# Two of four weight sums of a unit by accumulating transfers, and gelu as one function, in the projection stage of a one-core decoder layer

## The chip, the cores and the metric

The kernel runs on one core of a Trainium2 chip. The metric is the device time of one execution in microseconds; the median of three runs counts. Engines are named as in the profile: PE is TensorE, DVE VectorE, ACT ScalarE, POOL GpSimd, SP SyncE, which here only issues DMAs.

## The reference

One decoder layer for a prompt of 1024 rows and eight single decode rows, all float32, width 1024. What matters here is its first line and the recurrent branch:

```python
z = x @ w_in
xr, yr, q, k, v, xq, g = jnp.split(z, SPLIT_IDX, axis=-1)
xc, conv_new = causal_conv(xr, conv_buf, conv_w, conv_b)
hs, h_new = rg_lru(xc, h0, lru_wa, lru_ba, lru_wx, lru_bx, lru_lambda)
a_out = hs * jax.nn.gelu(yr, approximate=True)
```

`w_in` has 1024 rows and 7680 columns, cut among two halves of the recurrent branch (`xr`, `yr`), queries, keys and values of the window attention, queries of the memory attention, and three sets of gates. Two attention branches, the merge by gates, two layer norms and a gated feed-forward part follow; the change does not touch them.

## The kernel before

**Products.** Activations lie transposed: 1032 columns (1024 prompt rows and 8 decode rows) on 128 partitions by 8 blocks. Each float32 operand is split into a high and a low float32r part (`split`: a cast on ACT, then a subtraction on DVE), and each product is three matmuls (high by high, high by low, low by high).

**Units.** The first stage, `project`, works through 30 units (`UNITS`). A unit makes two blocks of 128 columns of `z` from two blocks of `w_in`, with seven products of half size where the plain way has eight. Its weights are four quarters, a11 and a12 (the halves of the first block, 128 x 512 each) and a21 and a22 (of the second). The seven weight operands, numbered 0 to 6, are

    0: a11          1: a21 + a22     2: (1) + a11    3: a12
    4: a11 + a21    5: (2) + a12     6: a22

So four of them (1, 2, 4, 5) are sums. `fast_load` loads the quarters of a unit from HBM on SP's queue (tiles `ur`), `fast_quarter` makes operand i (its sum into a tile `us`, on DVE, and its split into `u_ih` and `u_il`), and `fast_step` runs its 24 matmuls (two halves of the columns, four blocks, three matmuls each) into PSUM banks `ub`, `uc` or `ud` and copies the result out: `p1s`, `p5s` and `u2s` on ACT for i = 0, 1, 2, `za` and `zb` on DVE for i = 3, 4, 5, `zb` on ACT for i = 6. Operands 0, 2, 4, 6 add to the same bank `ub`, so step 2 starts only when `p1s` is copied, step 4 when `u2s` is, and step 6 when DVE has made `zb`.

**Order.** The loop in `project` asks for operand k + 3 at step k, three steps ahead. Loads of unit u + 1 are asked for in steps 1 to 3 of unit u. Behind each step, `pump` advances side work by a piece: the recurrent branch of a `lru` unit (`lru`: convolution, gates, a scan on DVE, gelu, a store to `scr_a`), memory attention of the decode rows (`dec_mem`: dot products `dcj` on DVE with tiles `dck`, `dcv` and broadcast rows `dckq`, `dcvq`), and others. From the seventh step on, a scheduler sets each engine's order by its own costs; before that it is as written. POOL has little to do in the stage: small copies of the recurrent branch (`pconv`, `scvo`, `pho`, `sho`) and one pass over `tr` per `lru` unit.

**Buffers.** Tiles `ur` have the tag `raw` with 6 buffers, tiles `us` the tag `sum` with 3 buffers in this stage (`sum_bufs`). A unit u > 1 is loaded in pieces (`staged`): two quarters at once, and the other two one by one by `fast_more`.

**Gelu.** `lru` writes gelu as y (1 + tanh(c (y + a y^3))) / 2 with a square and a tanh on ACT and three passes on DVE, the last of which multiplies with the scan's result.

Of the kernel before, what the change touches and what calls it, by code (L numbers as in the profile page):

```python
# [13 lines left out]
AF = mybir.ActivationFunctionType  # L14
ALU = mybir.AluOpType
# [5 lines left out]
D = 1024  # L21
# [29 lines left out]
SHARE = 0.5 / ALPHA  # L51
LN_EPS = 1e-5 / ALPHA ** 2
NEG = -1.0e30
GELU_C = math.sqrt(2.0 / math.pi)
GELU_A = math.sqrt(0.044715)

V_BG, V_CW, V_CB, V_BA, V_BX, V_LAM = 0, 24, 56, 64, 72, 80
V_G1, V_B1, V_G2, V_B2, V_SNK, V_SNKD, V_EPS, V_N = 88, 96, 104, 112, 120, 136, 137, 138
# [2 lines left out]
class Builder:  # L61
# [210 lines left out]

    def fast_load(self, u, src0, src1, staged=False):
        h = D // 2
        parts = [partial(self.half_raw, src[:, e * h:(e + 1) * h], h, f"ur{u}_{j}{e}")
                 for j, src in enumerate((src0, src1)) for e in range(2)]
        st = {"raw": [[f() for f in parts[:2]], []], "u": u, "more": deque(parts[2:])}
        if not staged:
            self.fast_more(st, 2)
        return st  # L280

    def fast_more(self, st, n):

        for _ in range(n):
            st["raw"][1].append(st["more"].popleft()())

    def sum_tile(self):

# [2 lines left out]
    def fast_quarter(self, st, i):  # L291

        nc, u = self.nc, st["u"]
        byhand = self.sfree is not None
        if byhand:
            a11, a12, a21, a22 = (st["r"].get(n) for n in (11, 12, 21, 22))
        else:
            a11, a12 = st["raw"][0]
            a21, a22 = st["raw"][1] or (None, None)
        if i in (1, 2, 4, 5):  # L300
            if byhand:
                src = st[2] if i == 5 else self.sum_tile()
            else:
                src = self.w1.tile([P, D // 2], F32, tag="sum", name=f"us{u}_{i}", bufs=self.sum_bufs)
            a, b = {1: (a21, a22), 2: (st.get(1), a11), 4: (a11, a21), 5: (st.get(2), a12)}[i]
            nc.vector.tensor_add(src, a, b)
            st[i] = src
        else:
            src = {0: a11, 3: a12, 6: a22}[i]
        if byhand and i == 2:  # L310
            self.sfree.append(st[1])
        if st.get("fifth") and i == 5:
            if not st["first"]:
                self.raw_done(st, 12)
            return
        hi, lo = self.half_pair(f"u{u}_{i}")
        self.split(hi, lo, src)
        if byhand and i in (4, 5):
            self.sfree.append(src)
        if byhand and i > 3:  # L320
            self.raw_done(st, *{4: (11, 21), 5: (12,), 6: (22,)}[i])
        st["q", i] = hi, lo
# [77 lines left out]
    def project(self, ctx, pool):  # L400

        nc, io, tc = self.nc, self.io, self.tc
        self.qdc = self.cst.tile([P, KT * NB], F32, name="qdc")
        self.qds = self.cst.tile([P, KT * NB], F32, name="qds")
        self.kd = self.cst.tile([P, 2 * NB], F32, name="kd")
        self.vd = self.cst.tile([NB, 256], F32, name="vd")
        self.lru_setup()
        self.side, self.pumped, self.late_gate = (deque(), deque()), 0, None
        n = len(UNITS)
        finish = [Finish(self, kind, j) for kind, j in UNITS]  # L410
        st = {}

        def load(u):
            a, b = finish[u].rows
            st[u] = self.fast_load(u, io["win"][a], io["win"][b], u > 1)

        ts = [[None] * 7, [None] * 7]
        for i in (6, 5, 2, 0, 1, 3, 4):
            for p in range(2):
                ts[p][i] = tuple(self.tp.tile([P, 4, QS], F32R, tag=f"t{i}", name=f"t{e}{i}_{p}", bufs=4) for e in "hl")  # L420
        todo = [(u, i) for u in range(n) for i in range(7)]
        ahead = 3
        xs = {}
        moving = self.combos(ts, xs)
        with tc.manual_schedule(engines=ORDERED):
            with pool("mx") as self.ph:
                self.mem_kv(moving, xs, lambda: load(0), [lambda i=i: self.fast_quarter(st[0], i) for i in range(2)])
            self.fast_quarter(st[0], 2)
            for k, (u, i) in enumerate(todo[:FIRST]):
                if i == 1:  # L430
                    load(u + 1)
                v, j = todo[k + ahead]
                if i == 1:
                    self.fast_step(st[u], i, ts, finish[u])
                if i != 2:
                    self.fast_quarter(st[v], j)
                if i == 2:
                    self.fast_step(st[u], i, ts, finish[u])
                next(moving, None)
                if k < 3:  # L440
                    next(moving, None)
                if i == 2:
                    self.fast_quarter(st[v], j)
                elif i != 1:
                    self.fast_step(st[u], i, ts, finish[u])
        assert next(moving, None) is None
        self.lr = ctx.enter_context(pool("lr"))
        self.dp = ctx.enter_context(pool("dp1"))
        with tc.issue_after(self.last_load):
            self.load_consts()  # L450
            self.load_lru()
        self.lru_consts()
        for k, (u, i) in enumerate(todo):
            if k < FIRST:
                continue
            if i == 1 and u + 1 < n:
                load(u + 1)
            if i in (2, 3) and u + 1 < n:
                self.fast_more(st[u + 1], 1)
            if k + ahead < len(todo):  # L460
                v, j = todo[k + ahead]
                self.fast_quarter(st[v], j)
            self.fast_step(st[u], i, ts, finish[u])
            self.pump()
            if i == 6:
                del st[u]
        while any(self.side):
            self.pump()
        nc.sync.dma_start(self.scr["c"][:, :, TP:T], self.cdec)
        self.store_lru()  # L470
        self.late_gate = None
# [491 lines left out]
    def lru(self, m, xr, yr):  # L963

        nc, io, vec = self.nc, self.io, self.vec
        col = lambda base: vec[:, base + m:base + m + 1]
        stt = nc.vector.scalar_tensor_tensor
# [17 lines left out]
        a, ti = self.zt(f"tr{m}"), self.zt(f"ti{m}")  # L985
        for c, (t0, n) in enumerate(THIRDS):
            x = [self.lr.tile([P, n], F32R, tag=f"xc{e}", name=f"xc{e}{m}_{c}", bufs=1) for e in range(2)]
            for e, r in enumerate(half):
                src = xc[r, t0:t0 + n]
# [18 lines left out]
        sq = self.zt(f"sq{m}")  # L1008
# [12 lines left out]
        nc.gpsimd.tensor_copy(self.sho[:, m, :], sq[:, TP:T])  # L1021
        yield
        g = self.zt(f"ge{m}")
        nc.scalar.activation(g, yr, AF.Square, scale=GELU_A)
        yield
        stt(g, g, 1.0, yr, op0=ALU.add, op1=ALU.mult)
        nc.scalar.activation(g, g, AF.Tanh, scale=GELU_C)
        yield
        stt(g, g, 1.0, yr, op0=ALU.add, op1=ALU.mult)
        yield  # L1030
        stt(g, sq, 0.5, g, op0=ALU.mult, op1=ALU.mult)
        nc.sync.dma_start(self.scr["a"][:, m, :], g)


# [318 lines left out]
    def plain(self, h):  # L1353

        ts = [[None] * 7, [None] * 7]
        steps = self.h_combos(h, ts)
        for f in range(PLAIN):
            self.plain_gate_up(f, h, steps)
        for _ in steps:
            pass  # L1360
        for p in range(2):
            ts[p][0], ts[p][3], ts[p][5] = h[p, 0], h[p, 1], h[2 + p, 1]
        return ts
# [699 lines left out]
class FinishDown:  # L2063


    scale = 1.0 / ALPHA
# [158 lines left out]
```

## Time and profile before

| what | value |
|---|---|
| time, median of 3 runs | 1877.86 us (1877.57 to 1879.27) |
| profiled execution, its own time | 1878.24 us |
| its span in the profile | 1876.5 us |
| granted TensorE clock, mean | 0.998 |
| PE busy | 1856.7 us, 99% of the span |
| DVE busy | 1443.0 us, 77% |
| ACT busy | 1055.0 us, 56% |
| POOL busy | 123.5 us, 7% |

Busy time is the union of an engine's instructions. PE's instructions overlap: a matmul of 128 x 258 is shown with some 0.28 us, and the next one starts 0.12 us after it. In a row of a group, the columns are line, engine, operation, output <- inputs, shape and count, then busy us, mean ns of one, and the engine's idle time just before them with what ended it. In a row of waits they are engine, line, what was waited for, us in total, how often, and the longest.

### The profile page before, as it was taken

The numbers are of one execution on the slowest core, as the hardware profiler recorded it, in microseconds if no ns is written. First come the engines' busy times: TensorE is split into PE (matmuls) and PEld (weight loads), VectorE is DVE, ScalarE is ACT, GpSimd is POOL, SyncE is SP. The second block draws the span as 40 slices with busy tenths as digits, with TensorE's granted clock in tenths as the row PEclk, the third lists the DMA queues.
The fourth block names the chain that finished last, engine by engine and source line by source line (L and its number), as shares of the span: only waits on it lengthen the run. The fifth ranks groups of instructions, "written<-read, shape, count | busy, mean of one in ns | idle before, by whom it ended". The sixth has DMA issues, their size and how long they took to land.

```text
span 1876.5 us, 38122 instructions
## 1 busy us (share of the span) xinstructions
PE 1856.7 (99%) x14616; PEld 1839.8 (98%) x14616; DVE 1443.0 (77%) x2932; ACT 1055.0 (56%) x2250; POOL 123.5 (7%) x187
## 2 busy tenths in 40 slices
PE   9999999999999999999999999999999999999998
PEld 9999999999999999999999999999999999999998
DVE  7878878888789757578887567798888787957486
ACT  6576676665666756568774234644443434735355
POOL 1000002110000000021210000000000000001100
PEclk9999999999999999999999999999999999999999
DMA  9535345447344368547535251255576566967862
GB/s 337 177 109 175 111 145 166 139 139 267 120 159 164 124 203 269 203 134 237 176 93 190 91 192 57 74 170 185 182 242 199 162 197 225 311 181 190 190 197 91
DMA packets 186678, 326.93 MB, mean 174 GB/s; under 512 B 19760, under 2 KB 97536, under 8 KB 186496
## 3 DMA queue, kind: packets, MB, share of 16 engines
q1 hardware_dynamic: 179392, 304.86, 49.4%
q0 software_dynamic: 4224, 14.78, 3.9%
q10 hardware_dynamic: 2880, 4.85, 0.7%
q8 instruction: 115, 1.88, 0.4%
q14 instruction: 67, 0.55, 0.1%
HBM read 238.76 MB, written 89.84 MB: 175 GB/s over the span
## 4 chain that ended last, share of the span: by engine, by line
PE 83%; DVE 6%; DMA 6%; issue 3%; ACT 2%; SPq 0%; POOL 0%; ACTq 0%; DVEq 0%; POOLq 0%
PE ub L332 5%; PE ub L334 5%; PE ub L333 5%; PE ubfg L332 3%; PE ubfg L334 3%; PE ubfg L333 3%; PE ud L334 2%; PE ud L333 2%; PE ud L332 2%; PE op L134 2%; PE op L136 2%; PE op L135 2%; PE brs L145 2%; PE brs L142 2%; PE brs L143 2%
## 5 line engine op out<-in xcount | busy, mean ns | idle before, releaser
L332 PE MATMUL ub<-th,u_6h 128*128 128x258 f32 x240 | 68.5, 285 | 1.4 <-DVE zb L380 1.1
L332 PE MATMUL ub<-th,u_2h 128*128 128x258 f32 x240 | 68.1, 284 | 0.8 <-ACT p1s L373 0.8
L332 PE MATMUL ub<-th,u_4h 128*128 128x258 f32 x240 | 68.2, 284 | 0.3 <-ACT u2s L373 0.3
L334 PE MATMUL ud<-th,u_5l 128*128 128x258 f32 x240 | 68.1, 284 | 0.0
L332 PE MATMUL ud<-th,u_1h 128*128 128x258 f32 x240 | 68.1, 284 | 0.0
L332 PE MATMUL ud<-th,u_5h 128*128 128x258 f32 x240 | 68.1, 284 | 0.0
L332 PE MATMUL ub<-th,u_0h 128*128 128x258 f32 x240 | 68.1, 284 | 0.0
L334 PE MATMUL ub<-th,u_6l 128*128 128x258 f32 x240 | 68.1, 284 | 0.0
L334 PE MATMUL ud<-th,u_1l 128*128 128x258 f32 x240 | 68.1, 284 | 0.0
L334 PE MATMUL ub<-th,u_0l 128*128 128x258 f32 x240 | 68.1, 284 | 0.0
L334 PE MATMUL ub<-th,u_2l 128*128 128x258 f32 x240 | 68.0, 284 | 0.0
L334 PE MATMUL ub<-th,u_4l 128*128 128x258 f32 x240 | 68.0, 284 | 0.0
L334 PE MATMUL uc<-th,u_3l 128*128 128x258 f32 x240 | 68.0, 284 | 0.0
L332 PE MATMUL uc<-th,u_3h 128*128 128x258 f32 x240 | 68.0, 283 | 0.0
L333 PE MATMUL ub<-tl,u_6h 128*128 128x258 f32 x240 | 67.7, 282 | 0.0
L333 PE MATMUL ub<-tl,u_0h 128*128 128x258 f32 x240 | 67.6, 282 | 0.0
L333 PE MATMUL ud<-tl,u_5h 128*128 128x258 f32 x240 | 67.6, 282 | 0.0
L333 PE MATMUL ub<-tl,u_4h 128*128 128x258 f32 x240 | 67.6, 282 | 0.0
L333 PE MATMUL ud<-tl,u_1h 128*128 128x258 f32 x240 | 67.6, 282 | 0.0
L333 PE MATMUL ub<-tl,u_2h 128*128 128x258 f32 x240 | 67.6, 282 | 0.0
L333 PE MATMUL uc<-tl,u_3h 128*128 128x258 f32 x240 | 67.6, 282 | 0.0
L134 PE MATMUL op<-mh,woh 128*128 128x258 f32 x224 | 63.4, 283 | 0.0
(1080 smaller groups left out, 8230.0 us busy)
## 6 DMA issues: line engine op xcount, KB each, us to landing
ur<-win SPq DMA_DIRECT2D x120, 256.0 KB, 3.0
raw<-wgu SPq DMA_DIRECT2D x80, 256.0 KB, 3.4
t<-scr_t SPq DMA_DIRECT2D x36, 516.0 KB, 4.0
z<-scr_f SPq DMA_DIRECT2D x28, 516.0 KB, 5.3
scr_f<-z SPq DMA_DIRECT2D x22, 516.0 KB, 2.9
scr_t<-z SPq DMA_DIRECT2D x20, 516.0 KB, 3.1
raw<-wdn SPq DMA_DIRECT2D x35, 256.0 KB, 5.4
z<-scr_t SPq DMA_DIRECT2D x16, 516.0 KB, 6.2
```

The source lines that it names most:

```text
L134: nc.tensor.matmul(ps, sh, mh, start=opens and i == 0, stop=False)
L135: nc.tensor.matmul(ps, sh, ml, start=False, stop=False)
L136: self.last_mm = nc.tensor.matmul(ps, sl, mh, start=False, stop=closes and i == last).ins
L142: mm(sh, mh, start=opens and i == 0, stop=False)
L143: mm(sl, mh, start=False, stop=False)
L145: self.last_mm = mm(sh, ml, start=False, stop=closes and i == len(terms) - 1).ins
L332: mm(sh[:, w], xh, start=opens and k == 0, stop=False)
L333: mm(sh[:, w], xl, start=False, stop=False)
L334: self.last_mm = mm(sl[:, w], xh, start=False, stop=k == 3).ins
```

## The change

For units 2 to 29, `fast_sums` replaces the loading. Operands 0, 3 and 6 are loaded as they are (a11, a12, a22). For operands 1 and 4 the first summand is loaded on SP's queue into a `sum` tile, and the second is added to it by an accumulating DMA on POOL's queue. Operands 2 and 5 are made by DVE in place in operand 1's tile, which is split again after each. a11, a21 and a22 are thus read twice from HBM. Loads are asked for in steps 1 to 4. The tile of operand 1 is held until operand 5 is split, that of operand 4 until its own split. Gelu is one function of ACT and one product on DVE.

```diff
     def fast_load(self, u, src0, src1, staged=False):
         h = D // 2
+        if staged:
+            return self.fast_sums(u, src0, src1)
...
+    def fast_sums(self, u, src0, src1):
+
+        h, nc = D // 2, self.nc
+        (a11, a12), (a21, a22) = ([src[:, e * h:(e + 1) * h] for e in range(2)] for src in (src0, src1))
+        raw = {}
+
+        def plain(k, src):
+            raw[k] = self.half_raw(src, h, f"ur{u}_{k}")
+
+        def both(k, a, b):
+            raw[k] = self.half_raw(a, h, f"us{u}_{k}", True)
+            nc.gpsimd.dma_start(raw[k], b, accum_op=ALU.add)
+
+        plain(0, a11)
+        both(1, a21, a22)
+        return {"sum": raw, "u": u, "more": deque((partial(plain, 3, a12), partial(both, 4, a11, a21), partial(plain, 6, a22)))}
...
     def fast_quarter(self, st, i):
 
         nc, u = self.nc, st["u"]
+        if "sum" in st:
+            raw = st["sum"]
+            if i in (2, 5):
+                nc.vector.tensor_add(raw[1], raw[1], raw[{2: 0, 5: 3}[i]])
+            hi, lo = self.half_pair(f"u{u}_{i}")
+            self.split(hi, lo, raw[{2: 1, 5: 1}.get(i, i)])
+            st["q", i] = hi, lo
+            return
...
-            if i in (2, 3) and u + 1 < n:
+            if i in (2, 3, 4) and u + 1 < n:
                 self.fast_more(st[u + 1], 1)
...
         g = self.zt(f"ge{m}")
-        nc.scalar.activation(g, yr, AF.Square, scale=GELU_A)
-        yield
-        stt(g, g, 1.0, yr, op0=ALU.add, op1=ALU.mult)
-        nc.scalar.activation(g, g, AF.Tanh, scale=GELU_C)
-        yield
-        stt(g, g, 1.0, yr, op0=ALU.add, op1=ALU.mult)
-        yield
-        stt(g, sq, 0.5, g, op0=ALU.mult, op1=ALU.mult)
+        nc.scalar.activation(g, yr, AF.Gelu_apprx_tanh)
+        yield
+        nc.vector.tensor_mul(g, sq, g)
         nc.sync.dma_start(self.scr["a"][:, m, :], g)
```

What the scheduler makes of it is shown at three places. A number behind a name is the unit or the branch's block, and the long number tells tiles of one name apart.

POOL's queue before, from the third to the fourth block of the recurrent branch (the copies stand behind the unit's `za` and the scan's `sq`):

```order
L1013 TENSOR_SCALAR tr2_3455<-th2_3854 128x1032
L1020 COPY pho_111<-sq2_3937 128x1
L1021 COPY sho_109<-sq2_3937 128x8
L979 COPY pconv_110<-za10_3997 128x3
L981 COPY scvo_107<-za10_3997 128x8
L1013 TENSOR_SCALAR tr3_4367<-th3_4774 128x1032
```

POOL's queue in the changed kernel at the same place, with the accumulating transfers (`us` <- `win`) of units 11 to 14 in it:

```order
L1047 COPY pho_111<-sq2_3836 128x1
L292 DMA us11_4_3974<-win 128x512
L1048 COPY sho_109<-sq2_3836 128x8
L292 DMA us12_1_4152<-win 128x512
L1006 COPY pconv_110<-za10_3981 128x3
L1008 COPY scvo_107<-za10_3981 128x8
L292 DMA us12_4_4241<-win 128x512
L292 DMA us13_1_4459<-win 128x512
L292 DMA us13_4_4548<-win 128x512
L292 DMA us14_1_4754<-win 128x512
L1040 TENSOR_SCALAR tr3_4233<-th3_4623 128x1032
```

The transfers now stand between the branch's copies, in POOL's one order. `us12_4` comes behind `pconv`, which waits for `za10`.

SP's queue in the changed kernel, where the tile of unit 12's operand 4 gets its first summand:

```order
L1054 DMA scr_a_69<-ge2_4010 128x1032
L1077 DMA dcvq2_1_4282<-dcpd1_3970 128x512
L103 DMA ur13_0_4457<-win 128x512
L1086 DMA dcv4_1_4364<-cmvT 128x2x256
L103 DMA ur13_3_4502<-win 128x512
L103 DMA us12_4_4241<-win 128x512
L1077 DMA dcvq4_1_4449<-dcpd1_3970 128x512
L1086 DMA dcv5_1_4451<-cmvT 128x2x256
L103 DMA us13_1_4459<-win 128x512
```

The load of `us12_4`, which waits for its buffer, stands behind two loads of unit 13; before, all quarters of unit 12 were issued ahead of those of unit 13.

ACT's order before, from the copies of unit 10 to those of unit 11, with the gelu of block 2 (two functions `ge2`) between them:

```order
L373 ACTIVATE u2s10_1_3974<-ub10_1_3875 128x258
L1094 ACT_TABLE_LOAD
L1094 ACTIVATE dcp1_3981,dcst1_3982<-dct1_3978,dcst1_3982 8x256
L84 CAST u11_1h_4065<-us11_1_4063 128x512
L1024 ACTIVATE ge2_4095<-zb7_3150 128x1032
L84 CAST u11_2h_4099<-us11_2_4097 128x512
L1027 ACTIVATE ge2_4095<-ge2_4095 128x1032
L84 CAST u11_3h_4131<-ur11_01_3899 128x512
L972 ACTIVATE xc3_4246<-za10_3997,vec_62 128x1032
L2095 ACTIVATE zb10_4031<-ub10_0_3860 128x258
L84 CAST u11_4h_4172<-us11_4_4170 128x512
L2095 ACTIVATE zb10_4031<-ub10_1_3875 128x258
```

ACT's order in the changed kernel at the same place:

```order
L400 ACTIVATE u2s10_1_3954<-ub10_1_3858 128x258
L1116 ACT_TABLE_LOAD
L1116 ACTIVATE dcp1_3964,dcst1_3965<-dct1_3961,dcst1_3965 8x256
L1051 ACT_TABLE_LOAD
L1051 ACTIVATE ge2_4010<-zb7_3141 128x1032
L82 CAST u11_1h_4047<-us11_1_3883 128x512
L82 CAST u11_2h_4078<-us11_1_3883 128x512
L82 CAST u11_3h_4114<-ur11_3_3921 128x512
L999 ACTIVATE xc3_4110<-za10_3981,vec_62 128x1032
L2117 ACTIVATE zb10_4018<-ub10_0_3843 128x258
L82 CAST u11_4h_4155<-us11_4_3974 128x512
L2117 ACTIVATE zb10_4018<-ub10_1_3858 128x258
```

The cast `u11_4h` stands at the same place, between the two copies `zb10`. A table load for gelu is added, and one function is gone. PE's order differs only inside this stage, by the places of the side work's matmuls.

More of the change, by code (lines that the diff above doesn't have):

```diff
@@ L53 @@
 NEG = -1.0e30
-GELU_C = math.sqrt(2.0 / math.pi)
-GELU_A = math.sqrt(0.044715)
 V_BG, V_CW, V_CB, V_BA, V_BX, V_LAM = 0, 24, 56, 64, 72, 80
@@ L277, in fast_load @@
         st = {"raw": [[f() for f in parts[:2]], []], "u": u, "more": deque(parts[2:])}
-        if not staged:
-            self.fast_more(st, 2)
-        return st
+        self.fast_more(st, 2)
+        return st
+    def fast_sums(self, u, src0, src1):
[10 more added lines that the diff above has]
+        return {"sum": raw, "u": u, "more": deque((partial(plain, 3, a12), partial(both, 4, a11, a21), partial(plain, 6, a22)))}
     def fast_more(self, st, n):
         for _ in range(n):
-            st["raw"][1].append(st["more"].popleft()())
+            if "sum" in st:
+                st["more"].popleft()()
+            else:
+                st["raw"][1].append(st["more"].popleft()())
     def sum_tile(self):
@@ L293, in fast_quarter @@
         nc, u = self.nc, st["u"]
+        if "sum" in st:
+            raw = st["sum"]
[5 more added lines that the diff above has]
+            return
         byhand = self.sfree is not None
```

## The prediction

> **What bounds the kernel now.** I read the page first, then the stage that the change touches as one window, then TensorE's own waits in it.
>
> ```profile
> span 1876.5 us, 38122 instructions
> PE 1856.7 (99%) x14616; PEld 1839.8 (98%) x14616; DVE 1443.0 (77%) x2932; ACT 1055.0 (56%) x2250; POOL 123.5 (7%) x187
> ```
>
> ```profile
> core 0: us, PE busy (x) PEld busy (x) DVE busy (x) ACT busy (x) POOL busy (x), PEclk, DMA share, GB/s
> 66.00:678.00 612.00, 609.07 (x5026) 606.97 (x5025) 494.77 (x1023) 396.30 (x754) 49.58 (x49) 1.00 0.46 153
> ```
>
> TensorE is busy 609.07 of the 612 us between the start of the steady stage and its end, at the full granted clock. That leaves 2.93 us. VectorE has 117 us free there and ScalarE 216 us. The change touches neither the number nor the shape of TensorE's instructions, so work that it takes off VectorE can be worth at most what TensorE waits for. Who it waits for, in the same window:
>
> ```profile
> PE ub L332 <- DVE zb L380: 1.1, 2, 0.8
> PE ub L332 <- ACT p1s L373: 0.8, 1, 0.8
> PE vt L497 <- ACT v L503: 0.5, 1, 0.5
> PE ub L332 <- ACT u2s L373: 0.3, 1, 0.3
> PE ub L332 <- DVE sq L1019: 0.3, 1, 0.3
> ```
>
> Six waits, 3.0 us together. Three of them (1.4 us) end with VectorE, three (1.6 us) with ScalarE. A wait costs a little more than its idle time, because matmuls overlap:
>
> ```profile
> 513.33 0.28 PE L333 MATMUL ud<-tl,u_5h 128*128 128x258 f32 x1
> 513.45 0.28 PE L334 MATMUL ud<-th,u_5l 128*128 128x258 f32 x1
> 514.51 0.39 PE L332 MATMUL ub<-th,u_6h 128*128 128x258 f32 x1 [0.79 <-DVE zb L380]
> ```
>
> Matmuls start 0.12 us apart; here 1.06 us passed, so 0.94 us were lost where 0.79 is shown as idle. With 0.15 us more for each of six waits, the whole stage holds 3.0 + 0.9 = 3.9 us that could be won. That is 0.2% of the time, about what a measurement of this kernel can tell from no change.
>
> **The change part by part.** First what leaves VectorE and ScalarE (rows of the same window, columns: busy us, mean ns of one):
>
> ```profile
> L306 DVE TENSOR_TENSOR us<-us,ur 128x512 f32<-128x512 f32 x59 | 40.5, 687 | 1.0
> L1029 DVE SCALAR_TENSOR_TENSOR ge<-ge,zb 128x1032 f32<-128x1032 f32 x8 | 9.8, 1223 | 0.0
> L85 DVE TENSOR_TENSOR tl<-x,th 128x1032 fp32r<-128x1032 f32 x2 | 2.5, 1226 | 0.0
> L1027 ACT ACTIVATE ge<-ge 128x1032 f32<-128x1032 f32 x8 | 8.5, 1068 | 11.1 <-DVE ge L1026 11.1
> L1009 ACT ACT_TABLE_LOAD x8 | 10.3, 1283 | 0.1
> ```
>
> *VectorE.* Units 2 to 29 lose two of four sums: 28 x 2 x 0.687 = 38.5 us. Each of eight gelus loses two of its three passes (the product that stays is of the size of the 1.226 us row): 8 x 2 x 1.223 = 19.6 us. The sums that stay, now in place, have the same two inputs and keep their 0.687. VectorE does 58 us less of 495. All of it lay beside TensorE's work except what stood before the three waits that end with VectorE; I take all three away: 1.4 + 3 x 0.15 = -1.9 us. If only some of the lateness was load, the gain is nearer 0.
>
> *ScalarE.* Each gelu loses one of two passes, 8 x 1.068 = -8.5 us. The gelu function brings its own function tables: the rows of the built programs hold 28 table loads in this stretch against 16, so 12 x 1.283 = +15.4 us, 6.9 us more in all, inside 216 us of idle time. It becomes visible only where ScalarE is late for a PSUM copy; of the p1s copies that happened to one (0.8 us). I take one more such wait, 0.8 + 0.15 = +0.9 us, between 0 and the second rival's bound.
>
> ```profile
> 267.80 0.63 ACT L84 CAST u_4h<-us 128x512 fp32r<-128x512 f32 x1
> 268.44 1.28 ACT L1009 ACT_TABLE_LOAD   x1
> 269.74 1.07 ACT L1009 ACTIVATE sq<-th 128x1032 f32<-128x1032 f32 x1
> ```
>
> A load here costs its 1.28 us and no more: it starts 0.01 us after the cast ends, and the next function starts 0.02 us after it. The Trainium skill (ScalarE: Activation LUTs, What ACT_TABLE_LOAD costs) gives about 2.66 us for each switch, since a drain of 1.38 us goes with the load. By that rule the 12 loads would be an estimated 32 us, still under ScalarE's idle time; the trace does not agree, and I go by the trace.
>
> *The transfers.* A unit had four loads of 256 KB on SP's queue. It now has five there and two accumulating ones on GpSimd's, each behind the load into the same tile.
>
> ```profile
> L105 SPq DMA_DIRECT2D ur<-win x120: 327/332/1372, 42.8 to 637.5; - x120
> ur<-win SPq DMA_DIRECT2D x112, 256.0 KB, 3.0
> L538 POOL DMA_DIRECT2D scr_mv<-mvr x8: 542/542/551, 38.6 to 56.3; - x8
> L2077 POOL DMA_DIRECT2D scr_h<-z x16: 858/882/1246, 1651.4 to 1799.9; - x16
> scr_mv<-mvr POOLq DMA_DIRECT2D x8, 128.0 KB, 2.4
> z<-scr_h POOLq DMA_DIRECT2D x8, 516.0 KB, 6.6
> DMA to landing us min/median/max: 5.3/7.5/13.2
> ```
>
> SP gets 28 issues more, 28 x 0.332 = 9 us over 612; nothing. GpSimd gets 56 at 0.54 to 0.88 us, about 40 us on an engine that is 8% busy. Per unit and sum tile the new chain is: tile free, SP issue 0.33, landing 3.0, GpSimd issue at most 0.88, landing X. No row shows X for 256 KB from HBM. From below it is 2.4 us (128 KB, no adding); from above 13.2 (the slowest transfer on scr_h, 516 KB). Nearest in kind are the eight transfers z<-scr_h, seven of which add in the same direction, with 6.6 us for twice the bytes; so I take 4.5, midway between 2.4 and 6.6, and the chain is 0.33 + 3.0 + 0.88 + 4.5 = 8.7 us.
>
> The time it has: the tile of a unit's fifth quarter (us_4) is freed by the split u_5l of the unit before, and is read by the cast u_4h. The rows of before show how far these two stand apart; the closest pair and a typical one:
>
> ```profile
> 527.42 0.68 DVE L85 TENSOR_TENSOR u_5l<-us,u_5h 128x512 fp32r<-128x512 f32 x1
> 538.38 0.62 ACT L84 CAST u_4h<-us 128x512 fp32r<-128x512 f32 x1 [0.87 <-PE ub L333]
> 292.46 0.67 DVE L85 TENSOR_TENSOR u_5l<-us,u_5h 128x512 fp32r<-128x512 f32 x1
> 305.35 0.61 ACT L84 CAST u_4h<-us 128x512 fp32r<-128x512 f32 x1
> ```
>
> These are 10.3 and 12.2 us from end to start; the 28 pairs of units 2 to 29, read off the same way, run from 10.3 to 18.9 with a median of 13.4. In the changed order the cast and the split keep these places among their PSUM copies. So the chain of 8.7 us is covered in every unit, and the transfer may land as late as 6.1 us after its issue before any cast waits. Behind a late cast stand the copies p1s of the next unit, which TensorE needs one step later: 24 matmuls of 0.12 us, 2.9 us. TensorE would notice from X = 9.0 us on. The other sum tile (us_1) is free a whole step group earlier and has more. I cost the transfers at 0.
>
> *GpSimd's queue.* The tile us_4 of every third unit is issued behind the copies pconv and scvo of the branch A chain, which wait for VectorE.
>
> ```profile
> L979 POOL COPY pconv<-za x8: 580/582/10913, 95.6 to 539.0; 128x3 f32<-128x3 f32 x8
> 283.69 10.91 POOL L979 COPY pconv<-za 128x3 f32<-128x3 f32 x1 [1.28 <-DVE za L383]
> ```
>
> One copy of eight took 10.9 us, and a transfer behind it would be held. But it ended at 294.6, and the tile of that unit was freed at 293.1 (the third row of the pairs) and could not be loaded before 293.1 + 0.33 + 3.0 = 296.5. Nothing is lost even in this worst case. The Trainium skill (SBUF — State Buffer, Who interferes with whom) has the rule that would speak against the change: VectorE instructions in a two-port mode lock GpSimd out, and with it the descriptors of its DMAs, and those with two SBUF inputs hold up only GpSimd's reads. The long copy fits the second half; the first is what the 0.54 us of all eight issues speaks against, for this kernel's instruction mix.
>
> *Bytes.* The stage moves 28 x 0.26 MB more on SP's queue and 14.7 MB on GpSimd's.
>
> ```profile
> q1 hardware_dynamic: 179392, 304.86, 49.4%
> q0 software_dynamic: 4224, 14.78, 3.9%
> ```
>
> That is 3.0 us per MB on the first (0.494 x 1876.5 / 304.86) and 5.0 on the second, so 22 + 73 = 95 us of all sixteen engines: the DMA share rises from 0.46 to about 0.61. Plain loads get slower by some tenths, for which the 1.6 us between 8.7 and 10.3 and the 2.9 behind it are the cover.
>
> **The sum.** The profiled execution took 1878.24 us (span 1876.5 and 1.7 around it), 0.4 above the median of the runs. 1878.2 - 1.9 + 0.9 + 0 = 1877.2; against the median 1876.9. What stands after the stage is in the same order on TensorE and keeps its time.
>
> **The rivals.**
> 1. *The accumulating transfers land late* (slower). Place: the cast u_4h at the head of ScalarE's queue, p1s behind it. It decides from X = 9.0 us. At X = 11 the chain is 15.2 us, 12.3 after the 2.9 us of cover; eight of the 28 pairs lie below and lose 8 us together: 1885. At 13.2, eighteen lose, 37 us: 1914. Against it: 6.6 us for twice the bytes. For it: a share of 0.61 and SP loads that queue ahead. Chance 0.13.
> 2. *ScalarE's table loads* (slower). If each of eight gelus makes one p1s copy as late as the one seen, 8 x 0.95 = 7.6 us: 1885. For it: loads now come twice in a short stretch. Against it: 216 us idle, and casts that wait for TensorE. Chance 0.10.
> 3. *VectorE's relief removes nearly all waits* (faster): -3.9 us, 1874.0. It needs the ScalarE waits to go as well. Chance 0.10.
> 4. *The sums were never on the path*, and the waits stay as they are, a little moved: 1878. It lies inside my forecast's range.
>
> **How the numbers follow.** The likeliest, waits going and coming within 3 us, has 0.67, for 1876.9, with its own range 1874.5 to 1881. The range from 1873.6 (all 3.9 won, and 0.4 of the runs' own spread) to 1885 takes in the second rival and the near end of the first, and leaves out the far end and what I don't see, some 0.15. Faster by over 0.2% (below 1874.1) 0.10, within 0.2% 0.68, slower (above 1881.6) 0.22.
>
> **What would show it.** Right: VectorE's busy time in the stage down by about 58 us and ScalarE's up by about 7, TensorE's idle time there still 1 to 4 us, q0 with 14.7 MB more, casts u_1h and u_4h waiting for TensorE and not for a transfer. Wrong: a row in which u_4h waits for us<-win for microseconds at a time (first rival), waits of ub for p1s or u2s behind table loads (second), a window of TensorE without idle time (third), or VectorE's dots on the memory branch, which now stand earlier in its queue, waiting for dcvq or dckq ahead of a PSUM copy.

## The result and the profile after

The changed kernel takes 1888.87 us (1884.93 to 1892.67, four runs), beside 1877.71 us for the kernel before (1877.03 to 1879.27, four runs). The ratio is 1.0053, 95% interval 1.0037 to 1.0069: slower by half a per cent, 11 us, where 1876.9 was forecast. The profiled execution took 1888.56 us. Its page begins:

```profile
span 1886.8 us, 38293 instructions
PE 1859.5 (99%) x14616; PEld 1840.1 (98%) x14616; DVE 1395.2 (74%) x2860; ACT 1061.7 (56%) x2254; POOL 149.2 (8%) x243
```

VectorE is busy for 47.8 us less, and the kernel is longer all the same. The loss lies in the stage that was changed. The stage as one window, first of before, then of the changed kernel (columns as in the prediction's window):

```profile
66.00:690.00 624.00, 620.70 (x5107) 618.27 (x5106) 503.20 (x1040) 405.37 (x773) 49.58 (x49) 1.00 0.46 153
```

```profile
66.00:690.00 624.00, 612.89 (x5046) 609.81 (x5046) 448.64 (x954) 402.09 (x758) 76.13 (x106) 1.00 0.64 186
```

TensorE was idle for 3.3 us of 624 before, and for 11.1 us now. The same matmul behind the stage, first before, then in the changed kernel:

```profile
685.77 0.45 PE L145 MATMUL bra<-baL,wba_h 128*128 128x384 f32 x1 [0.37 <-DVE baL L85]
```

```profile
694.99 0.44 PE L143 MATMUL bra<-baL,wba_h 128*128 128x384 f32 x1 [0.37 <-DVE baL L83]
```

It starts 9.2 us later, which is most of the 10.3 that the span is longer. What TensorE waits for in that window of the changed kernel, in place of the six short waits of before:

```profile
PE ub L359 <- DVE zb L407: 8.1, 7, 2.4
PE g L1023 <- DVE za L405: 2.0, 2, 1.8
PE ub L359 <- ACT u2s L400: 0.6, 2, 0.3
PE ub L359 <- ACT p1s L400: 0.4, 1, 0.4
```

Of these 11.1 us, 10.1 end with VectorE, 8.1 of them with `zb`, although VectorE is less busy. So the next view is what VectorE itself waits for. Its dots of the memory branch (`dcj`) wait for their broadcast rows (`dckq`, `dcvq`) and for tiles of values (`dcv`), first before, then in the changed kernel:

```profile
DVE dcj L1070 <- DMA dckq<-dcq: 8.9, 6, 2.1
DVE dcj L1070 <- DMA dcvq<-dcpd: 6.8, 4, 2.8
DVE dcj L1070 <- DMA dcv<-cmvT: 0.2, 1, 0.2
```

```profile
DVE dcj L1092 <- DMA dckq<-dcq: 21.1, 10, 3.7
DVE dcj L1092 <- DMA dcvq<-dcpd: 7.9, 6, 2.9
DVE dcj L1092 <- issue: 7.0, 2, 4.8
DVE dcj L1092 <- DMA dcv<-cmvT: 1.7, 1, 1.7
```

These are 15.9 us in 11 waits before and 37.7 us in 19 now; for 7.0 of the 37.7, marked `issue`, the profile shows no cause. One of them in order of time, VectorE and TensorE in the changed kernel:

```profile
95.92 0.43 DVE L1092 SCALAR_TENSOR_TENSOR dcj<-dck,dckq 128x256 f32<-128x256 f32 x1 [3.22 <-DMA dckq<-dcq]
96.27 0.08 DVE L1092 DVE_READ_ACCUMULATOR dcj<-dck,dckq 128x1 f32 x1
96.27 0.42 DVE L407 SCALAR_TENSOR_TENSOR zb<-ub,p5s 128x258 f32<-128x258 f32 x1
...
96.74 0.39 PE L359 MATMUL ub<-th,u_6h 128*128 128x258 f32 x1 [2.35 <-DVE zb L407]
```

The dot waits 3.2 us for its row. The PSUM copy `zb` stands right behind it in VectorE's queue, and step 6 cannot start before `zb`: TensorE loses 2.35 us. The five next longest waits at step 6 (at 243.6, 310.0, 374.8, 523.5 and 587.7 us) each have a dot that waited shortly ahead of `zb`: it starts 0.4 to 3.2 us before it. Not all of them waited for a row: the dot at 309.2 us waited for its tile of values, and the one at 584.0 us is one of the two marked `issue`.

### The profile page after: what moved, and what is told of

Read it like the earlier page. It is cut to its first block, busy times and chain, and to the rows that moved or that the text cites. A ratio compares the mean times of both kernels' runs of the same rounds, so it can differ in the third digit from the quotient of the medians.

```text
span 1886.8 us, 38293 instructions
## 1 busy us (share of the span) xinstructions
PE 1859.5 (99%) x14616; PEld 1840.1 (98%) x14616; DVE 1395.2 (74%) x2860; ACT 1061.7 (56%) x2254; POOL 149.2 (8%) x243
## 4 chain that ended last, share of the span: by engine, by line
PE 65%; DMA 4%; DVE 4%; ACT 3%; issue 1%; SPq 0%; POOL 0%; DVEq 0%; ACTq 0%
PE ubfg L359 3%; PE ubfg L361 3%; PE ubfg L360 3%; PE ub L359 2%; PE ub L361 2%; PE ub L360 2%; PE op L132 2%; PE ubf L359 2%; PE op L134 2%; PE op L133 2%; PE brs L143 2%; PE ubf L360 2%; PE brs L140 2%; PE brs L141 2%; PE ubf L361 2%; PE bra L143 1%
## 5 line engine op out<-in xcount | busy, mean ns | idle before, releaser
L292 POOL DMA_DIRECT2D us<-win x56 | 49.7, 898 | 353.7 <-DVE u_5l L83 76.3
L2099 POOL DMA_DIRECT2D scr_h<-z x16 | 14.3, 914 | 738.5 <-DVE uf_3l L83 659.9
```

The costliest lines, as they stand in the source:

```text
L292: nc.gpsimd.dma_start(raw[k], b, accum_op=ALU.add)
L2099: self.b.nc.gpsimd.dma_start(self.b.scr["h"][:, m, :], z, accum_op=ALU.add)
```

## The experiments

Three theories stood at the start. A: the change lets VectorE's scheduler pull the dots further ahead, where their rows are not there yet. In the built programs, 43 of the 64 pairs of dots stand earlier against the operands' splits than before, 9 later, on average by 1.6 operands of a unit's seven. B: the accumulating transfers make the rows land later. C: the function tables of gelu make ScalarE late. The kernel before was run again on the same chip each time, at 1878.4 to 1878.7 us. In the table, "stage" is the time from the `u2s` wait at about 67 us (step 4 of the window's first unit) to the first wait of a `bra` matmul (the one shown above), and "dots" is what the dots wait in 66 to 690 us, the waits marked `issue` included, both in the one profiled execution; "traffic" means the accumulating transfers.

| kernel | median us | ratio (95%) | stage | dots |
|---|---|---|---|---|
| before | 1877.7 | 1 | 619.1 | 15.9 |
| changed | 1888.9 | 1.0053 (1.0037 to 1.0069) | 628.7 | 37.7 |
| gelu alone | 1879.3 | 1.0006 (0.9994 to 1.0018) | 618.7 | 18.5 |
| sums alone | 1891.4 | 1.0063 (1.0047 to 1.0080) | 631.7 | 30.4 |
| changed, plain second transfer | 1883.6 | 1.0027 (1.0016 to 1.0037) | 621.4 | 29.6 |
| changed, no second transfer | 1878.5 | 0.9997 (0.9988 to 1.0005) | 616.2 | 21.0 |
| before + spare traffic | 1882.0 | 1.0017 (1.0007 to 1.0027) | 621.4 | 18.2 |
| before, dots held | 1874.3 | 0.9976 (0.9967 to 0.9984) | 614.8 | 1.7 |
| gelu alone, held | 1875.0 | 0.9979 (0.9970 to 0.9989) | 614.8 | 2.5 |
| before + spare traffic, held | 1874.1 | 0.9971 (0.9961 to 0.9982) | 615.2 | 1.4 |
| changed, no second, held | 1877.0 | 0.9987 (0.9978 to 0.9997) | 614.9 | 1.5 |
| changed, held | 1875.4 | 0.9986 (0.9977 to 0.9996) | 617.3 | 2.9 |
| changed, held, again | 1875.6 | 0.9985 (0.9976 to 0.9993) | 616.4 | 4.5 |

**Gelu alone, and the sums alone.** Each half of the change by itself. Gelu alone is the kernel before with

```diff
-        nc.scalar.activation(g, yr, AF.Square, scale=GELU_A)
-        yield
-        stt(g, g, 1.0, yr, op0=ALU.add, op1=ALU.mult)
-        nc.scalar.activation(g, g, AF.Tanh, scale=GELU_C)
-        yield
-        stt(g, g, 1.0, yr, op0=ALU.add, op1=ALU.mult)
-        yield
-        stt(g, sq, 0.5, g, op0=ALU.mult, op1=ALU.mult)
+        nc.scalar.activation(g, yr, AF.Gelu_apprx_tanh)
+        yield
+        nc.vector.tensor_mul(g, sq, g)
```

and the sums alone are the changed kernel with these lines put back.

> The gelu of the change alone, with all four sums on VectorE and the loads of before. Theory A (order): with less work on VectorE the scheduler pulls the dot products of the memory branch (dcj) further ahead of their place, in front of PSUM copies, where they wait for their broadcast rows (dckq, dcvq); gelu takes a third of the 58 us off VectorE, so about a third of the +11 us: 1881, between 1878 and 1884. Theory B (traffic): the accumulating transfers load the DMA engines, the rows land later, and that is what stops VectorE; gelu alone adds no traffic: 1878. Theory C (function tables on ScalarE): all of the +11 us: 1888, with TensorE waiting for p1s or u2s.

> The sums of the change alone, with gelu as before. Theory A (order): two thirds of the relief, so two thirds of the loss: 1885, between 1881 and 1888. Theory B (traffic): all of it, 1888. Theory C (function tables): none of it, 1878.

Gelu alone: 1879.32 us, no measurable difference, which fits theory B and the low end of theory A. The sums alone: 1891.4 us, the whole loss and by the median 2.5 us more, above what either theory gave. Theory C falls: the table loads come with gelu, and gelu shows no cost.

**The changed kernel with held dots.** Each dot is ordered behind VectorE's last PSUM copy of steps 3 to 5 as the program is written, by an edge that sets the queue's order and adds no wait on another engine. The traffic stays as it is.

```diff
-                add(st["za"][:, cols(0, p)], c, in1=st["s", 0, p])
+                self.last_evac = add(st["za"][:, cols(0, p)], c, in1=st["s", 0, p]).ins
...
-                nc.vector.scalar_tensor_tensor(junk, ...)
+                ins = nc.vector.scalar_tensor_tensor(junk, ...).ins
+                self.behind(ins, self.last_evac)
```

> The changed kernel, with each dot product of the memory branch held behind the PSUM copy that VectorE made last when the dot was written in the program (an order on VectorE's own queue, no new wait between engines). Theory A (order): the dots no longer stand in front of copies with their transfers still under way; TensorE's idle time in the stage falls from 11 us to 2 to 4, the time to 1878 to 1880. Theory B (traffic): the rows land as late as before; the dots wait less since they stand later, so some comes back, but plain loads stay slow: 1882 to 1888. Theory C: 1888.

1875.42 us, ratio 0.9986: the loss is gone, and a little more; every theory had expected at least 1878. Its window of the stage, and what the dots and TensorE's step 6 wait for in it:

```profile
66.00:690.00 624.00, 621.43 (x5119) 619.97 (x5118) 453.20 (x972) 415.27 (x779) 76.42 (x106) 1.00 0.66 189
```

```profile
DVE dcj L1092 <- DMA dckq<-dcq: 2.9, 2, 2.5
```

```profile
PE ub L359 <- DVE zb L407: 1.3, 1, 1.3
```

The DMA share there is 0.66, no less than in the changed kernel. The dots stand five operands later than in the kernel before (mean of the 64 pairs in the built program 4.8), and all but two rows have landed by then. So the loss passes through the dots; this run does not tell whether order or traffic put them in the way.

**A plain transfer in place of the adding one.** The second transfer overwrites its tile, so 56 additions are left out; every order and every byte stays.

```diff
-            nc.gpsimd.dma_start(raw[k], b, accum_op=ALU.add)
+            nc.gpsimd.dma_start(raw[k], b)
```

> The changed kernel, but the second transfer into a sum tile on GpSimd's queue overwrites the first and does not add, so that these two operands are not sums (this leaves out 56 additions in the DMA engines and keeps every transfer, wait and place). Theory A (order): the same order of VectorE's instructions, so about the same loss: 1886 to 1889. Theory B (traffic): q0 takes the engines for 3.0 us per MB or so and not 6; half or more of the loss goes: 1878 to 1883. Theory C: 1888.

1883.63 us, just above theory B's range: 5.0 of the 11 us are left. Landing, and GpSimd's queue in the window 66 to 690 us, first adding, then plain:

```profile
us<-win POOLq DMA_DIRECT2D x56, 256.0 KB, 5.0
q0 software_dynamic: 8064, 14.68, 14.7%
```

```profile
us<-win POOLq DMA_DIRECT2D x56, 256.0 KB, 3.7
q0 software_dynamic: 4480, 14.68, 7.4%
```

The same 14.68 MB takes twice the time of the DMA engines when it adds. How much the transfers load the engines thus counts, against theory A alone.

**No second transfer at all.** Operands 1 and 4 hold only their first summand. VectorE's and ScalarE's orders are row for row those of the changed kernel.

```diff
-            nc.gpsimd.dma_start(raw[k], b, accum_op=ALU.add)
```

> The changed kernel without the accumulating transfers: operands 1 and 4 hold only their first summand, so 56 additions are left out. VectorE's and ScalarE's orders are row for row those of the changed kernel; the traffic of GpSimd's queue is gone. Theory A (the order alone): 1885 to 1889, as the changed kernel. Theory B (the traffic alone): 1877 to 1878.5, with rows landing in 3.7 us again. Both needed together: 1879 to 1883, at or below the run with plain transfers (1883.6).

1878.51 us, ratio 0.9997: the changed order costs nothing by itself. Theory A falls as it stood. The place of the example above is here the same in every row but the landing. Its row is the third `dckq`, issued at 89.8 us in both kernels. SP's and GpSimd's queues in the changed kernel, then SP's and VectorE's here:

```profile
89.82 0.33 SPq L1077 DMA_DIRECT2D dckq<-dcq  x1
89.87 0.88 POOL L292 DMA_DIRECT2D us<-win  x1 [4.19 <-DVE dcj L1092]
```

```profile
89.81 0.33 SPq L1076 DMA_DIRECT2D dckq<-dcq  x1
...
93.43 0.43 DVE L1091 SCALAR_TENSOR_TENSOR dcj<-dck,dckq 128x256 f32<-128x256 f32 x1 [0.76 <-DMA dckq<-dcq]
93.78 0.09 DVE L1091 DVE_READ_ACCUMULATOR dcj<-dck,dckq 128x1 f32 x1
93.78 0.42 DVE L406 SCALAR_TENSOR_TENSOR zb<-ub,p5s 128x258 f32<-128x258 f32 x1
```

Without the accumulating transfer, which is issued 0.05 us behind it in the changed kernel, the dot has its row 3.6 us after the issue; with it, after 6.1 us (with a plain second transfer, 5.9). `zb` comes 2.5 us earlier here, and TensorE has no wait at that place. In the whole window:

```profile
DVE dcj L1091 <- DMA dckq<-dcq: 9.8, 9, 2.2
```

```profile
PE ub L358 <- DVE zb L406: 0.3, 1, 0.3
```

But theory B's sign, rows that land in 3.7 us again, did not show: where the profile gives a landing (three rows each), the median of `dckq` is 5.2 us here and 5.3 in the changed kernel. Of the 32 rows, 14 end a wait of their first dot in both kernels. Ten of these come within 0.7 us of each other, counted from their issue; three come 1.2 to 2.5 us later in the changed kernel, and one comes 1.4 us earlier. The longest wait there (3.7 us, at 373.5 us) is for a further row that comes at least 3.1 us later. Most of the 16.7 us that the dots wait more stand at six of the 32 rows, and two kinds of lateness can be told apart: a row that needs longer, as above, and a row that is asked for later. For the second kind, the 8 KB store `dcpd` from which the first row of a group is read, and that row's issue, in the changed kernel and then here:

```profile
281.31 0.29 SPq L1120 DMA_DIRECT2D dcpd<-dcp  x1
285.61 0.35 SPq L1077 DMA_DIRECT2D dcvq<-dcpd  x1
```

```profile
278.16 0.29 SPq L1119 DMA_DIRECT2D dcpd<-dcp  x1
279.48 0.35 SPq L1076 DMA_DIRECT2D dcvq<-dcpd  x1
```

The row can be asked for 4.3 us after the store's issue in the changed kernel and 1.3 us after it here; its dot waits 2.9 us there and not at all here.

**Spare traffic in the kernel before.** The first try asked for too much of one buffer: a plain load of 192 KB on SP's queue and three accumulating transfers, all into one spare tile.

```diff
+            return st
+        t = self.dp.tile([P, 384], F32, tag="xtra", name=f"xt{u}", bufs=1)
+        self.nc.sync.dma_start(t, src0[:, :384])
+        st["xtra"] = lambda o, w: self.nc.gpsimd.dma_start(t[:, :w], src1[:, o:o + w], accum_op=ALU.add)
+        st["xtra"](0, 384)
...
+                st[u + 1]["xtra"](*{2: (384, 384), 3: (768, 256)}[i])
```

> The kernel before, with the changed kernel's traffic added but none of its arithmetic moved: each of units 2 to 29 also loads 192 KB on SP's queue into a spare tile and adds 512 KB to it by three accumulating transfers on GpSimd's queue; nobody reads the tile. VectorE's order is that of before but for one place of some 20 rows at units 4 to 6. Theory A (the order alone): as before, 1878 +- 1. Theory B (the traffic alone makes the rows dckq and dcvq land later): 1885 to 1889. Both needed together: rows land about a microsecond later, dots wait some 20 instead of 16 us, 1879 to 1882.

2019.53 us, far outside every expectation, and for a reason of its own. SP's queue and GpSimd's waited for the spare tile, in 66 to 830 us:

```profile
SPq L282 <- DMA xt<-win: 300.1, 31, 14.1
```

```profile
POOL xt L283 <- DMA xt<-win: 349.0, 81, 8.5
```

The loads of the weights stand behind it on SP's queue, and TensorE was busy for 502.6 us of the 624 from 66 to 690 us. The run tells nothing of the traffic. The second try has no load on SP's queue, and two transfers of 192 KB a unit, each behind a copy of one column that holds it to its time:

```diff
+        self.xtra = self.dp.tile([P, 384], F32, tag="xtra", name="xtra", bufs=1)
+        nc.gpsimd.memset(self.xtra, 0.0)
...
+            if i in (1, 4) and u + 1 < n:
+                nc.gpsimd.tensor_copy(self.xtra[:, :1], st[u + 1]["raw"][i // 4][1][:, :1])
+                nc.gpsimd.dma_start(self.xtra, io["win"][finish[u + 1].rows[0]][:, (i == 4) * 384:(i == 4) * 384 + 384], accum_op=ALU.add)
```

> The kernel before, with two accumulating transfers of 192 KB a unit on GpSimd's queue into one spare tile that nobody reads (three quarters of the changed kernel's accumulating bytes; a copy of one column from the newest quarter holds each transfer to its time). VectorE's order is that of before but for two neighbouring rows, ScalarE's and SP's are the same row for row. The changed order without the traffic took 1878.5, so the order alone costs nothing. Theory AB (the traffic delays the rows, and any order in which dots stand right ahead of PSUM copies turns the delay into stalls): dots of before already wait 15.9 us, so 1881 to 1886. Theory A' (the traffic hurts only with the dots as far ahead as in the changed kernel): 1878 to 1879.5, with dots waiting some 20 us but no new wait of TensorE for zb.

1882.01 us, ratio 1.0017: in the time that theory AB gave. So the traffic costs something with the order of before too. But its profile, one of its fastest executions (1880.39 us), does not show AB's way to it: the dots wait only 2.3 us more, and TensorE's waits for `zb` fell.

```profile
PE ub L332 <- ACT p1s L373: 1.5, 2, 0.8
PE uc L332 <- ACT v L508: 1.0, 1, 1.0
PE vt L502 <- ACT v L508: 0.9, 1, 0.9
PE ub L332 <- DVE zb L380: 0.5, 2, 0.3
```

Most of them end with ScalarE. One of the two `p1s` waits can be followed: a dot waits for its row on VectorE, the copy `za` behind it is late, ScalarE's gate function waits for `za`, and `p1s` stands behind that.

```profile
245.01 0.43 DVE L1075 SCALAR_TENSOR_TENSOR dcj<-dck,dckq 128x256 f32<-128x256 f32 x1 [2.12 <-DMA dckq<-dcq]
245.82 1.16 ACT L2106 ACTIVATE za<-za,hbg 128x1032 f32<-128x1032 f32 x1 [3.90 <-DVE za L383]
250.66 0.39 PE L332 MATMUL ub<-th,u_2h 128*128 128x258 f32 x1 [0.72 <-ACT p1s L373]
```

The two waits that end with `v` (1.9 us together) have another last link: by the profile, ScalarE's copies of `v` right ahead of them wait 0.3 and 0.2 us for stores to HBM (`scr_vd`, `scr_g`) to land, and not for VectorE. The rest of these two waits and the other `p1s` wait were not traced.

**The same kernels with held dots.** The hold of above, put into before, into before with the spare traffic, into the changed kernel without its second transfer, into before with gelu alone, and the changed kernel with held dots once more.

> The kernel before, with nothing of the change in it, and each dot product dcj ordered behind VectorE's last PSUM copy, as in the run that undid the loss. Dots of before waited 15.9 us for their rows in the stage, 1.1 us of that showed as TensorE waiting for zb. Theory A (the order of the dots decides): these go, 1876 to 1878, and the changed kernel with held dots (1875.4) is then better than this one only by what VectorE's lighter load is worth. If holding alone is worth the whole gain, this run gives 1875.4 too and the change itself is worth nothing. If holding the dots costs something when VectorE is fuller, 1879 or more.

> The run with the spare transfers, and each dot ordered behind VectorE's last PSUM copy besides. Both theories: the stalls go, and what is left against before with held dots (1874.3) is what the traffic costs by other ways than the dots: 1874 to 1876. If GpSimd's own work (tr, which VectorE waits for) suffers from standing behind transfers, 1877 or more.

> The changed kernel without the accumulating transfers (56 additions are left out) and with held dots: VectorE's lighter load alone, with the stalls on rows taken away on both sides. Against before with held dots (1874.3): if the lighter load is worth the 1.9 us that the prediction gave it, 1872.4; if the sums were never on the path, 1874.3; if ScalarE's table loads and the cast behind the sum in place cost more than the load saves, 1875.5, which would then explain all of what the changed kernel with held dots (1875.5) lacks, and the traffic nothing.

> The kernel before with gelu as one function and held dots, the likely best of the parts. If gelu's lighter load on VectorE is worth anything once the dots no longer stall: 1873 to 1874. If the table loads cost what the passes save: 1874.3, as with held dots alone. If the 0.4 to 0.6 us by which gelu alone was over before is real: 1874.9.

> The changed kernel with held dots once more, beside the kernel before with held dots on the same chip, to see which of the two is better and whether it beats the kernel before by more than its runs spread. Theory A: 1875.4 again, 0.1% below before. If the first result was chance: 1877 to 1878.

Held dots alone make the kernel before faster, 1874.29 us and 0.9976, below every value that was expected. TensorE's waits of the stage in that run, the first two of which begin and end it:

```profile
PE bra L145 <- DVE baL L85: 0.4, 1, 0.4
PE ub L332 <- ACT u2s L373: 0.3, 1, 0.3
```

No others are left. Spare traffic on top shows no cost (0.9971), though without the hold it cost 0.17%: so the hold takes away what the traffic cost there. That it all went by way of the dots is not shown, since two of the waits have stores as their last link.

With held dots, VectorE's lighter load wins nothing in the stage: it takes 614.8 us before, 614.8 with gelu alone and 614.9 with the whole relief and no traffic. The whole time of that last run, 1877.0 us, lies above all three values that were expected of it. Its profiled execution is 2.6 us longer than that of before with held dots, and 2.0 of these lie behind the stage. What stands behind the stage takes 1189.0 to 1192.7 us in the thirteen profiled executions of the table, so differences of this size in the whole time need not come from the stage; their cause was not looked for.

The changed kernel with held dots (0.9986, 0.9985) is not better than the kernel before with held dots (0.9976); the intervals overlap, so that it is worse is not shown. Its stage is 1.5 to 2.5 us longer in two profiled executions. The versions to keep are before with held dots, or that with gelu as one function (0.9979), both faster than both kernels.

**What follows.** Most of the loss needs two things at once. With the changed order and no second transfer the time is that of before; with three quarters of the accumulating bytes in the order of before it is 3.6 us more; with both 11 us more; and with the dots held there is no loss. Within the changed order the sizes hang together: the dots wait 21.0, 29.6 and 37.7 us with no, a plain and an adding second transfer, and the medians rise with them, 1878.5, 1883.6 and 1888.9. Across orders they do not: before with spare traffic loses 3.6 us with 18.2 us of dots' waits, and the sums alone lose more than the whole change with 30.4.

For the sums alone (1891.4 against 1888.9 us; the intervals of the ratios overlap) the profile shows one wait that the changed kernel does not have, and that passes by no dot. ScalarE's copy of `v` waits for a store of `zb` to land, and TensorE for the copy:

```profile
453.77 0.37 ACT L532 COPY v<-vt 128x256 f32<-128x256 f32 x1 [2.37 <-DMA scr_g<-zb]
454.19 0.33 PE L526 MATMUL vt<-ident,za 128*128 128x128 f32 x1 [2.77 <-ACT v L532]
```

Its 2.8 us are about what the two stages differ by (631.7 and 628.7). So the dots are the main way by which transfers reach TensorE here, and not the only one.

What stays open: how much of the changed kernel's loss is due to its extra plain bytes on SP's queue, what the waits marked `issue` wait for, and why only some rows and stores land late.

## Why the prediction was wrong

**The step that failed** is the cover under *Bytes*: "Plain loads get slower by some tenths, for which the 1.6 us between 8.7 and 10.3 and the 2.9 behind it are the cover." Two things are wrong with it. The size was short in places: `ur` landed in 3.9 us (median) where 3.0 was the row, though 0.6 of these 0.9 us are there without the second transfer too (3.6). The row of the example needed 6.1 us where 3.6 were enough without it, and an 8 KB store 4.3 us where it needed 1.3. And the cover belongs to the weights only. The rows `dckq` and `dcvq` use the same queues and have no such cover: there are two buffers, so a row is asked for when a dot frees one (the first of a group when its small store has landed), and the next dot that needs it stands a few microseconds on in VectorE's queue, with `zb` behind it. What is queued behind a waiting instruction was asked of ScalarE's casts and of GpSimd's copies, and not of VectorE's dots. They appear only in the last clause of what would show it wrong, "VectorE's dots on the memory branch, which now stand earlier in its queue, waiting for dcvq or dckq ahead of a PSUM copy". That is what happened, but it had no price and no chance of its own. The working put it at nothing; TensorE lost 10.1 us to VectorE in the stage, where it had lost 1.4.

**The term of -1.9 us** for VectorE's relief is not settled. With the relief and no second transfer, TensorE's waits of the window are 1.0 us together where before they were 3.4, and the stage of the profiled execution is 2.9 us shorter (616.2 and 619.1), more than the term asks; the whole time stays (1878.5), since in that execution 1.2 us more lie ahead of the stage and 2.0 more behind it. But load was not the only cause of these waits: held dots remove them with VectorE as full as before, and then 49 us less of VectorE's busy time (505 and 456 in the window) move the stage by 0.1 us. The relief itself was put at 58 us, a sum of durations; busy time is a union, and neighbouring instructions overlap at their ends.

**The ceiling** was nearly right. It allowed 3.9 us for all of TensorE's waits in the stage. Held dots win 4.3 us of the stage (619.1 to 614.8) and 4.4 us of the time. The gain was there, but another edit takes it.

**The transfers** were right for their own consumers. X was taken as 4.5 us and is 5.0 (median; 8.4 at most, where 9.0 was the limit), and no cast waits for one, so the first rival falls. What was not foreseen is that the sum in place ties ScalarE's cast `u_2h` to VectorE; TensorE's waits that end with ScalarE stay at 1.0 us all the same:

```profile
ACT u_2h L82 <- DVE us L316: 62.2, 18, 10.9
```

The price of 5.0 us per MB for the adding queue was low: 0.147 x 624 / 14.68 = 6.2. The share of 0.61 came out as 0.64.

**ScalarE** was right in its load (1055.0 to 1061.7, 6.7 us where 6.9 was worked out) and its price of 0.9 us is too small to be told: gelu alone shows no loss, with or without held dots, within intervals of some 0.1% to either side. The second rival, 7.6 us, falls. Its table loads took 1.28 us each in the trace before, and nothing here speaks for the longer switch that the prediction set aside.

**GpSimd's queue** took its 56 issues at 0.90 us each, 49.7 us where some 40 were worked out, and TensorE did not notice:

```profile
L292 POOL DMA_DIRECT2D us<-win x56 | 49.7, 898 | 353.7 <-DVE u_5l L83 76.3
```

**The third rival** falls for the change as it is. Without the second transfer most of TensorE's waits did go (3.4 to 1.0 us), most of those that end with ScalarE too, but the time did not follow.

**The range** ended at 1885.0, at the size of a single rival. A rival "rows of the dots land late" could have been priced from rows at hand: dots waited in 11 places before, and if each waited one microsecond more ahead of a PSUM copy, the end is some 11 us later, 1889 by that estimate. That it meets the measured time is chance: the dots' waits grew by 21.8 us, and TensorE's waits by 7.8.

## What to carry to other kernels

When a change adds transfers, look not only at the consumers of those transfers: list every load on the machine that is asked for just in time (few buffers, freed by its own consumer), and what stands behind its consumer in that engine's queue. An engine that waits in order for a transfer is late whatever its load, so a busy share that falls is no evidence that its waits fall; hold such consumers behind the copies that TensorE needs, which in the kernel before won 0.24%. And test order and traffic apart: each alone looked harmless or small.

## What the runs showed of the hardware

In these runs an adding float32 transfer from HBM to SBUF takes the DMA engines twice as long as a plain one of the same bytes: 14.7% against 7.4% of the engines' time in the window for 14.68 MB, that is 6.2 and 3.1 us of all sixteen engines per MB, in 8064 packets against 4480; it lands in 5.0 against 3.7 us for 256 KB.

In the run whose queues were stuck there are stretches in which TensorE idled for a third of the time, and its granted clock was lower there; one of them:

```profile
400.00:500.00 100.00, 65.65 (x491) 64.54 (x490) 42.24 (x76) 42.03 (x77) 19.37 (x24) 0.81 0.57 146
```

The clock is 0.81 where it is 1.00 in the busy stage. A matmul takes 0.134 us of busy time in this row (65.65 / 491) and 0.122 us in the stage of before (620.70 / 5107), so part of the 141 us by which that run was longer than before is slower matmuls and not only waiting.
